# A hybrid decoder layer on one core: other banks and pools at the change from the attention loop to the merged projections, and the first fast pair as fourth unit

## The chip, the cores and the metric

The kernel runs on 1 core of one Trainium2 chip. The metric is the device time of one execution in microseconds. Before the change the median of 3 runs is 1044.36 us (1043.06 to 1044.58). The execution that the profiler recorded took 1042.83 us; its trace spans 1041.1 us from the first to the last instruction.

## The reference

One layer on 256 tokens of width 2048, all in float32. The input is normalised and projected to everything that follows; two token mixers, a 16-head latent attention and a short gated convolution, are widened by SiLU gates, projected back, weighted by two sigmoid gates that come from the input, added, and sent through one output projection:

```
h = _rmsnorm(x, pre_norm_g);  proj = h @ w_in      # q_a, c_kv, k_rope, z_mla, c_in, b_gate, c_gate, z_conv, g_mla, g_conv
attn   = causal_mla_attention(q, k, v) * silu(z_mla)
conv   = sum(conv_w[k] * u_pad[:, k:k + s] for k in range(3)),   u = c_gate * c_in
y_mla  = attn @ w_o_mla
y_conv = (b_gate * conv * silu(z_conv)) @ w_o_conv
merged = sigmoid(g_mla) * y_mla + sigmoid(g_conv) * y_conv
x + _rmsnorm(merged @ w_out, post_norm_g)
```

The change lies where the loop over heads ends and the four products with `g_mla`, `g_conv`, `w_o_mla` and `w_o_conv` begin. These four form the merged stage.

## The kernel before, in words

**Split operands.** Every float32 operand is used as two parts, a high part `hi` in the fast matmul format and the rest `lo`. A product of two such operands takes three matmuls (`product`, L262): hi by hi, hi by lo, lo by hi. The high part of a weight is a copy on ACT (`whi`), the low part a subtraction on DVE (`wlo`); both stand in `split_act` (L279). So TensorE (PE) waits for ACT and DVE, never for a transfer directly.

**Units.** The weights come in units of 1 MB in the order of a list. `load_raw` puts a unit in one of three `raw` tiles by a transfer on SP's queue, `split_unit` splits it, and `take(i)` runs loads three and splits one unit ahead. The split halves live in rings of five tiles each, `whi` and `wlo`; a unit takes two of each, so the copy of a later unit's half waits until PE has read an older one. ACT and DVE work strictly in the order in which their instructions stand. That order is set by a scheduler that gets the program as written, with the pools' overlaps as dependencies; transfers and PE's matmuls keep the program's order.

**The end of the loop over heads.** The last convolution block goes through a turn: DVE transposes a tile into `cw` or `mv2x`, POOL's queue writes it to `far` in DRAM and reads it back into `cv_f` (`turned`, L352; `channels_join`). These late transfers are still under way when the merged stage begins. The last head's values are summed in the bank with the tag "o" (`o15`), which DVE empties at L432 (`whole`), and the last convolution block in the two banks "cv".

**The merged stage.** It has four products n = 0..3 (two gates, two outputs), each in two column blocks c of eight pairs k of 128-row slices. A plain pair is four results by two slices, 8 products or 24 matmuls. Blocks with n < 2 go through `fast_block` (L1005), in which the pairs in `FAST = (0, 3, 5)` are computed in Strassen-Winograd form with 7 products, 21 matmuls, from sums of the operands: `split_seven` (L216) makes sums of the weights on DVE (`ts`, L222) and splits them (`th` on ACT, `tl` on DVE); `mixed(k)` (L984) makes sums of the normalised input (`xr` and `xm` on DVE, L988 and L992), split into `mix`. `first_sums` empties the banks that only fast pairs use (p1, q5, q7, q6), `last_sums` the others (p2, q3, q4, d22). The order of the first block is `pair_order[0, 0]` (L142): two plain pairs, 1 and 2, and then pair 0 as third unit.

**Space.** `bp`, the pool of the head loop, is closed (L949) and `sp` is opened over the same addresses: gates `g`, `mix`, the rings `ts`, `th`, `tl` and `ev` (whose tiles also hold `xr` and `xm`). A tile of `sp` may be written only when what lay there before is done. In the kernel before, the gates of n = 1 cover the two `cw` tiles and the `tl` ring covers `mv1x` and `mv2x`, the tiles of the late transfers.

In tile names the number behind `raw`, `whi`, `wlo`, `ts`, `th`, `tl` is that of the unit: 113 and 114 are the first two of the merged stage (pairs 1 and 2), 115 the third and so on.

Of the kernel before, what the change touches and what calls it, by code (L numbers as in the profile page):

```python
# [18 lines left out]
P = 128  # L19
S = 256  # L20
NT = S // P
D = 2048
# [62 lines left out]
def tile_layer(ctx: ExitStack, tc: tile.TileContext, xw, w0, xb, x, pos, pvec, post_g, wc, wz, wcv, wkr, wqk, wqr, wv, cwr, wd, wo, out):  # L85
# [53 lines left out]
            u_head[i][j] = add(wcv[i, j])  # L139

    pair_order = {(n, c): list(range(PAIRS)) for n in range(4) for c in range(2)}
    pair_order[0, 0] = [1, 2, 0, 4, 3, 6, 5, 7]  # L142
    u_d, seven = {}, set()
    for n in range(4):
        for c in range(2):
            for k in pair_order[n, c]:
                u_d[n, c, k] = add(wd[n, c, k])
                if n < 2 and k in FAST:
                    seven.add(u_d[n, c, k])

    out_order = [(c, k) for c in range(3) for k in range(2)] + [(c, k) for c in range(3) for k in (2, 3)]
# [64 lines left out]
    def split_seven(i, t):  # L216
        hi, hi2 = (wpool.tile([P, HALF], F32R, name=f"whi{i}_{j}", tag="whi", bufs=5) for j in range(2))
        lo, lo2 = (wpool.tile([P, HALF], F32R, name=f"wlo{i}_{j}", tag="wlo", bufs=5) for j in range(2))
        ta, tb = (sp.tile([P, HALF], F32, name=f"ts{i}_{j}", tag="ts", bufs=2) for j in range(2))
        ha, hb = (sp.tile([P, HALF], F32R, name=f"th{i}_{j}", tag="th", bufs=2) for j in range(2))  # L220
        la, lb = (sp.tile([P, HALF], F32R, name=f"tl{i}_{j}", tag="tl", bufs=2) for j in range(2))
        plus = lambda o, a, b: nc.vector.tensor_tensor(o, a, b, op=ALU.add)  # L222
# [36 lines left out]
    def bank(name, tag="mm", bufs=4):  # L259
        return psum.tile([P, 512], F32, name=name, tag=tag, bufs=bufs)  # L260
# [65 lines left out]
    bstack = main.enter_context(ExitStack())  # L326
# [17 lines left out]
    def temp(name, shape=(P, S), dt=F32, bufs=2, tag=None):  # L344

        tag, n = tag or name.rstrip("0123456789_"), shape[-1]
        if n % LINE == 0:
            return bp.tile(list(shape), dt, name=name, tag=tag, bufs=bufs)
        return bp.tile([P, -(-n // LINE) * LINE], dt, name=name, tag=tag, bufs=bufs)[:, :n]


# [597 lines left out]
    bstack.close()  # L949
    spool = ctx.enter_context(ExitStack())  # L950
    sp = spool.enter_context(tc.tile_pool(name="sp", bufs=1))
    gate = [[sp.tile([P, D], F32, name=f"g{n}_{t}") for t in range(NT)] for n in range(2)]
    mix = {k: sp.tile([P, 2, 4 * P], F32R, name=f"mix{k}") for k in FAST}

    def at_place(k):
        return x_both, k
# [25 lines left out]
            split_turned(src[:, c, t, :], place, c, t)  # L982

    def mixed(k):  # L984
        tmp = sp.tile([P, R], F32, name=f"xr{k}", tag="ev", bufs=2)
        f = tmp[:, :].rearrange("p (j s) -> p j s", j=2)
        ks = slice(2 * k, 2 * k + 2)
        nc.vector.tensor_tensor(f, x_both[:, ks, :S].bitcast(F32), x_both[:, ks, S:].bitcast(F32), op=ALU.add)  # L988
        raw = sp.tile([P, R], F32, name=f"xm{k}", tag="ev", bufs=2)
        a11, a21, a12, a22 = (f[:, j, t * P : (t + 1) * P] for j in range(2) for t in range(2))  # L990
        m7, m5, m6, m3 = (raw[:, j * P : (j + 1) * P] for j in range(4))
        minus = lambda o, a, b: nc.vector.tensor_tensor(o, a, b, op=ALU.subtract)  # L992
# [10 lines left out]
        return slice((2 * c + j) * R, (2 * c + j + 1) * R)  # L1003

    def fast_block(n, c, part, outs, between):  # L1005
        q = {name: bank(f"{name}_{n}{c}") for name in ("p1", "q5", "q7", "q6")}
        q["p2"] = bank(f"p2_{n}{c}", tag="st", bufs=1)
        q["q3"] = bank(f"q3_{n}{c}", tag="o", bufs=1)
        q["q4"], q["d22"] = (bank(f"{name}_{n}{c}", tag="cv", bufs=2) for name in ("q4", "d22"))
        order = pair_order[n, c]  # L1010
        calls = []
        for k in order:
            if k in FAST:
                for name, a, b in (
                    ("p1", part(2 * k, 0), "b11"), ("q5", mix_part(k, 1), "t1"), ("q7", mix_part(k, 0), "t3"),
                    ("q6", mix_part(k, 2), "t2"), ("p2", part(2 * k + 1, 0), "b21"), ("q3", mix_part(k, 3), "b22"),
                    ("q4", part(2 * k + 1, 1), "t4"),
                ):
                    calls.append((k, name, a, b))
            else:  # L1020
                for name, t, j in (("p2", 0, 0), ("q3", 0, 1), ("q4", 1, 0), ("d22", 1, 1)):
                    for i in range(2):
                        calls.append((k, name, part(2 * k + i, t), {(0, 0): 0, (1, 1): 1, (1, 0): 2, (0, 1): 3}[i, j]))
        firsts, lasts = {}, {}
        for at, (k, name, a, b) in enumerate(calls):
            firsts.setdefault(name, at)
            lasts[name] = at
        t_a, t_b = (sp.tile([P, R], F32, name=f"ev{i}_{n}{c}", tag="ev", bufs=2)[:, :] for i in range(2))
        (o11, o12), (o21, o22) = outs
        tt = lambda o, a, b, op=ALU.add: nc.vector.tensor_tensor(o, a, b, op=op)  # L1030

        def first_sums():
            nc.scalar.activation(t_a, q["p1"][:, :], AF.Copy)
            tt(t_b, q["q6"][:, :], t_a, ALU.subtract)
            tt(o12, q["q5"][:, :], t_b)
            tt(o21, q["q7"][:, :], t_b)
            tt(o22, q["q5"][:, :], o21)

        def last_sums():
            tt(o11, q["p2"][:, :], t_a)  # L1040
            tt(o12, q["q3"][:, :], o12)
            tt(o21, q["q4"][:, :], o21, ALU.subtract)
            tt(o22, q["d22"][:, :], o22)

        at = 0
        for i, k in enumerate(order):
            w = take(u_d[n, c, k])
            if i == order.index(max(FAST)) + 1:
                first_sums()
            between(i)  # L1050
            while at < len(calls) and calls[at][0] == k:
                _, name, a, b = calls[at]
                product(q[name][:, :], a, w[b] if k in FAST else w(b, R), firsts[name] == at, lasts[name] == at)
                at += 1
        last_sums()

    def plain_block(n, c, part, between):
        tags = ("mm",) * 4 if c == 0 else ("st", "o", "cv", "cv")
        q = {
            (t, j): bank(f"sq{n}{c}_{t}{j}", tag=tag, bufs={"mm": 4, "cv": 2}.get(tag, 1))  # L1060
            for (t, j), tag in zip(((0, 0), (0, 1), (1, 0), (1, 1)), tags)
        }
        order = pair_order[n, c]
        for at, k in enumerate(order):
            w = take(u_d[n, c, k])
# [10 lines left out]

    make_identity(nc, ident[:, :])
    for n in range(2):
        for c in range(2):

            def between(i):
                if n == c == 0 and i < 2:
                    for k in FAST[i : i + 1] if i == 0 else FAST[1:]:
                        mixed(k)
                if n == c == 1 and i in (2, 4, 6):
                    split_group(at_place, at_t, i // 2 - 1)

# [39 lines left out]
        for t in range(NT):  # L1127
            out_product(pss[t], t, w, kk)

    pss = [[bank(f"out{c}_{t}") for t in range(NT)] for c in range(2)]  # L1130
    pss.append([bank(f"out2_{t}", tag="cv", bufs=2) for t in range(NT)])
    for i, (c, kk) in enumerate(out_order[:6]):
        w = take(u_out[c, kk])
        if i == 5:
# [189 lines left out]
```

## Time and profile before

| | |
|---|---|
| median of the runs | 1044.36 us (1043.06 to 1044.58, 3 runs) |
| profiled execution | 1042.83 us, span 1041.1 us |
| busy share of the span | PE 98%, DVE 72%, ACT 52%, POOL 17% |
| mean granted TensorE clock | 0.993 |
| the chain that ended last | PE 97%, DVE 1% |

PE is busy to nine tenths or more in each of the page's 40 slices but two: the last (8 tenths) and one in the middle, from about 599 to 625 us (6 tenths), whose granted clock is 7 tenths. The merged stage begins at 590.09 us. "Idle before" in a row is the time in which the engine stood still ahead of an instruction; a matmul's row has its modelled length, and the distance between the starts of two rows is what it costs.

### The profile page before, as it was taken

How to read it: one execution, taken by the hardware profiler on the slowest of the kernel's cores; microseconds unless marked ns; L12 is line 12 of the kernel's file. 1: busy time of each engine (PE TensorE's matmuls, PEld its weight loads, DVE VectorE, ACT ScalarE, POOL GpSimd, SP SyncE). 2: the span in 40 equal slices, each digit the busy share in tenths (PEclk: the TensorE clock that was granted, in tenths of full speed). 3: DMA queues.
4: the chain of work that ended last, by engine and by line, in shares of the span. 5: the costliest groups of instructions: out<-in, count | busy, mean ns of one | idle time of the engine just before them, and what ended most of it. 6: DMA issues, size and time to landing. Idle time of an engine off the chain costs nothing.

```text
span 1041.1 us, 12831 instructions
## 1 busy us (share of the span) xinstructions
PE 1022.9 (98%) x4648; PEld 851.5 (82%) x4648; DVE 752.3 (72%) x1067; ACT 546.5 (52%) x766; POOL 179.8 (17%) x344
## 2 busy tenths in 40 slices
PE   9999999999999999999999969999999999999998
PEld 8888888888888888888888748888888888888886
DVE  7588777787777877777777789898975554657572
ACT  7666545555555555564555446555654343343451
POOL 4640421204211133012233110000000000214000
PEclk9999999999999999999999979999999999999999
DMA  9775876567665586656777635565645555577852
GB/s 358 281 246 213 273 223 226 203 213 270 228 234 208 206 265 225 248 212 204 267 241 259 226 122 196 204 218 190 229 173 198 202 195 184 207 263 252 327 189 81
DMA packets 44527, 233.26 MB, mean 224 GB/s; under 512 B 7952, under 2 KB 10512, under 8 KB 21552
## 3 DMA queue, kind: packets, MB, share of 16 engines
q1 hardware_dynamic: 32400, 199.67, 53.9%
q0 software_dynamic: 11632, 29.48, 8.8%
q10 hardware_dynamic: 432, 3.29, 0.8%
q8 instruction: 36, 0.59, 0.2%
q14 instruction: 27, 0.22, 0.1%
HBM read 215.66 MB, written 12.58 MB: 219 GB/s over the span
## 4 chain that ended last, share of the span: by engine, by line
PE 97%; DVE 1%; ACT 0%; DMA 0%; issue 0%; DVEq 0%
PE cv L90 34%; PE sq L90 17%; PE q L90 9%; PE z L90 8%; PE out L90 8%; PE p L90 4%; PE d L90 3%; PE qa L90 2%; PE kn L90 2%; PE qn L90 2%; PE vv L90 2%; PE ckv L90 2%; PE sc L90 1%; PE qr L90 1%; PE o L90 1%; PE kr L90 0%
## 5 line engine op out<-in xcount | busy, mean ns | idle before, releaser
L281 DVE TENSOR_TENSOR wlo<-raw,whi 128x1024 fp32r<-128x1024 f32 (+1 forms) x370 | 431.2, 1178 | 205.3 <-ACT whi L280 198.1
L280 ACT ACTIVATE whi<-raw 128x1024 fp32r<-128x1024 f32 (+1 forms) x372 | 373.1, 1020 | 375.7 <-PE cv L90 115.3
L90 PE MATMUL cv<-whi,x_both 128*128 128x512 f32 x1024 | 319.8, 389 | 0.0
L90 PEld LDWEIGHTS cv<-whi,x_both 128*128 128x128 f32 x1024 | 192.3, 188 | 39.5
L90 PE MATMUL cv<-wlo,x_both 128*128 128x512 f32 x512 | 199.5, 390 | 0.0
L90 PE MATMUL sq<-whi,x_both 128*128 128x512 f32 x384 | 118.7, 389 | 0.0
L90 PEld LDWEIGHTS cv<-wlo,x_both 128*128 128x128 f32 x512 | 96.1, 188 | 19.3
L90 PEld LDWEIGHTS sq<-whi,x_both 128*128 128x128 f32 x384 | 72.1, 188 | 15.0
L90 PE MATMUL z<-whi,x_both 128*128 128x512 f32 x256 | 80.0, 389 | 0.0
L90 PE MATMUL out<-whi,x_both 128*128 128x512 f32 x256 | 79.0, 389 | 0.0
L364 POOL DMA_DIRECT2D far<-g x32 | 17.5, 553 | 332.0 <-DVE g L1115 300.3
L90 PE MATMUL sq<-wlo,x_both 128*128 128x512 f32 x192 | 74.7, 389 | 0.0
L364 POOL DMA_DIRECT2D far<-via x64 | 35.3, 558 | 179.6 <-DVE via L356 179.6
L90 PEld LDWEIGHTS out<-whi,x_both 128*128 128x128 f32 x256 | 48.0, 188 | 10.1
L90 PEld LDWEIGHTS z<-whi,x_both 128*128 128x128 f32 x256 | 48.1, 188 | 9.9
L90 PE MATMUL q<-whi,x_both 128*128 128x512 f32 x160 | 52.6, 390 | 2.6 <-DVE f L432 2.6
L90 PE MATMUL z<-wlo,x_both 128*128 128x512 f32 x128 | 49.8, 389 | 0.0
L90 PE MATMUL out<-wlo,x_both 128*128 128x512 f32 x128 | 49.8, 389 | 0.0
L90 PE MATMUL p<-whi,x_both 128*128 128x512 f32 x128 | 47.0, 393 | 0.0
L90 PEld LDWEIGHTS sq<-wlo,x_both 128*128 128x128 f32 x192 | 36.0, 188 | 7.5
L364 POOL DMA_DIRECT2D far<-cw x48 | 26.2, 553 | 78.6 <-DVE cw L356 78.6
L90 PE MATMUL sq<-whi,cv_first 128*128 128x512 f32 x128 | 39.7, 389 | 0.0
(253 smaller groups left out, 1443.6 us busy)
## 6 DMA issues: line engine op xcount, KB each, us to landing
raw<-wcv_dram SPq DMA_DIRECT2D x64, 1024.0 KB, 5.6
raw<-wd_dram SPq DMA_DIRECT2D x64, 1024.0 KB, 4.8
raw<-wz_dram SPq DMA_DIRECT2D x16, 1024.0 KB, 4.8
raw<-wo_dram SPq DMA_DIRECT2D x16, 1024.0 KB, 4.8
raw<-wqk_dram SPq DMA_DIRECT2D x8, 1024.0 KB, 6.0
cw<-cwr_dram POOLq DMA_DIRECT2D x24, 256.0 KB, 6.2
raw<-wc_dram SPq DMA_DIRECT2D x4, 1024.0 KB, 9.7
raw<-wv_dram SPq DMA_DIRECT2D x4, 1024.0 KB, 4.9
```

The costliest lines, as they stand in the source:

```text
L90: return tc.keep_in_program_order(nc.tensor.matmul(*a, **kw))
L280: a = nc.scalar.activation(hi, src, AF.Copy)
L281: b = nc.vector.tensor_tensor(lo, src, hi.bitcast(F32), op=ALU.subtract)
L364: tc.keep_in_program_order(queue.dma_start(out=f[i], in_=m))
```

## The change

It does five things.

1. **Banks.** In `fast_block` the results p2, q3, q4 and d22, which plain pairs use, go to the four "mm" banks, and p1, q5, q7, q6 to "st", "o" and the two "cv". The plain blocks and the output blocks swap their banks to match.
2. **Order of the first block.** `pair_order[0, 0]` becomes 1, 2, 4, 0, 6, 3, 5, 7: pair 0 is the fourth unit, pair 3 the sixth.
3. **One fast pair less.** In that block pair 5 is plain: 24 matmuls where there were 21, and no `ts`, `th`, `tl` for it.
4. **Places.** `cw`, `mv1x` and `mv2x` get a pool `lp` of their own at the end of the space. In `sp` the rings `ts`, `th` and `ev` come first, over `qa`, `ckv` and other tiles that are done long before, the `tl` ring over tiles of the head loop. `g1_1` is opened over `lp` only at n = 1.
5. **Sums of the input.** `mixed` is called for pairs 0, 3, 5 at units 1, 3, 5 of the first block, where it was at units 0 and 1.

```diff
-    pair_order[0, 0] = [1, 2, 0, 4, 3, 6, 5, 7]
+    pair_order[0, 0] = [1, 2, 4, 0, 6, 3, 5, 7]
+    fast = {(n, c): FAST if n < 2 else () for n in range(4) for c in range(2)}
+    fast[0, 0] = FAST[:2]
...
-        ta, tb = (sp.tile([P, HALF], F32, name=f"ts{i}_{j}", tag="ts", bufs=2) for j in range(2))
+        ta, tb = (sums(f"ts{i}_{j}") for j in range(2))
...
+    lp = lstack.enter_context(tc.tile_pool(name="lp", bufs=1, side="right"))
...
-            return bp.tile(list(shape), dt, name=name, tag=tag, bufs=bufs)
+            return (lp if tag in ("cw", "mv1x", "mv2x") else bp).tile(list(shape), dt, name=name, tag=tag, bufs=bufs)
...
-    gate = [[sp.tile([P, D], F32, name=f"g{n}_{t}") for t in range(NT)] for n in range(2)]
-    mix = {k: sp.tile([P, 2, 4 * P], F32R, name=f"mix{k}") for k in FAST}
+    for r in (sums, sums_hi, evens):
+        r("home")
+    gate = [[None] * NT for _ in range(2)]
+    gate_tile(1, 0)
+    mix = {k: sp.tile([P, 2, 4 * P], F32R, name=f"mix{k}") for k in FAST[::-1]}
+    sums_lo("home")
+    for t in range(NT):
+        gate_tile(0, t)
...
-        q = {name: bank(f"{name}_{n}{c}") for name in ("p1", "q5", "q7", "q6")}
-        q["p2"] = bank(f"p2_{n}{c}", tag="st", bufs=1)
-        q["q3"] = bank(f"q3_{n}{c}", tag="o", bufs=1)
-        q["q4"], q["d22"] = (bank(f"{name}_{n}{c}", tag="cv", bufs=2) for name in ("q4", "d22"))
+        q = {name: bank(f"{name}_{n}{c}") for name in ("p2", "q3", "q4", "d22")}
+        q["p1"] = bank(f"p1_{n}{c}", tag="st", bufs=1)
+        q["q5"] = bank(f"q5_{n}{c}", tag="o", bufs=1)
+        q["q7"], q["q6"] = (bank(f"{name}_{n}{c}", tag="cv", bufs=2) for name in ("q7", "q6"))
...
-        tags = ("mm",) * 4 if c == 0 else ("st", "o", "cv", "cv")
+        tags = ("mm",) * 4 if c else ("st", "o", "cv", "cv")
...
+        if n:
+            lstack.close()
+            last_gate = spool.enter_context(tc.tile_pool(name="last_gate", bufs=1))
+            gate[1][1] = last_gate.tile([P, D], F32, name="g1_1")
...
-                if n == c == 0 and i < 2:
-                    for k in FAST[i : i + 1] if i == 0 else FAST[1:]:
-                        mixed(k)
+                if n == c == 0 and i in (1, 3, 5):
+                    mixed(FAST[i // 2])
...
-    pss = [[bank(f"out{c}_{t}") for t in range(NT)] for c in range(2)]
-    pss.append([bank(f"out2_{t}", tag="cv", bufs=2) for t in range(NT)])
+    pss = [[bank(f"out0_{t}", tag=tag, bufs=1) for t, tag in enumerate(("st", "o"))]]
+    pss += [[bank(f"out1_{t}", tag="cv", bufs=2) for t in range(NT)], [bank(f"out2_{t}") for t in range(NT)]]
```

Two places show how the instructions move. The first is ACT from the last convolution copy to the first `mix`, which PE waits for. Before, unit 115 is pair 0 (fast), 116 pair 4, 117 pair 3:

```order
L431 ACTIVATE half_5535<-o15_5529 128x256
L280 ACTIVATE whi115_1_5628<-raw115_5582 128x512
L280 ACTIVATE whi116_0_5692<-raw116_5625 128x1024
L280 ACTIVATE whi116_1024_5696<-raw116_5625 128x1024
L280 ACTIVATE whi117_0_5723<-raw117_5690 128x1024
L280 ACTIVATE th115_0_5633<-ts115_0_5631 128x1024
L280 ACTIVATE th115_1_5634<-ts115_1_5632 128x1024
L280 ACTIVATE mix0_5565<-xm0_5594 128x512
```

With the change unit 115 is pair 4 (plain), 116 pair 0 (fast), 117 pair 6, 118 pair 3:

```order
L434 ACTIVATE half_5538<-o15_5532 128x256
L282 ACTIVATE whi115_1024_5628<-raw115_5588 128x1024
L282 ACTIVATE whi116_0_5667<-raw116_5622 128x1024
L282 ACTIVATE whi116_1_5668<-raw116_5622 128x512
L282 ACTIVATE whi117_0_5714<-raw117_5665 128x1024
L282 ACTIVATE th116_0_5673<-ts116_0_5671 128x1024
L282 ACTIVATE whi117_1024_5718<-raw117_5665 128x1024
L282 ACTIVATE whi118_0_5754<-raw118_5712 128x1024
L282 ACTIVATE th116_1_5674<-ts116_1_5672 128x1024
L282 ACTIVATE mix0_5570<-xm0_5634 128x512
```

The two sums' copies stood together behind the first half of the unit after next; now two copies of later units stand between them, and `mix0` is behind all four.

The second place is DVE at the same point. Before, from the last low parts ahead of the sums of pair 0 to the first sum of the next fast pair; `xr3` and the low part of `mix0` follow:

```order
L281 TENSOR_TENSOR wlo116_1024_5697<-raw116_5625,whi116_1024_5696 128x1024
L281 TENSOR_TENSOR wlo117_0_5725<-raw117_5690,whi117_0_5723 128x1024
L988 TENSOR_TENSOR xr0_5592<-x_both_104 128x512
L222 TENSOR_TENSOR ts115_0_5631<-raw115_5582 128x1024
L992 TENSOR_TENSOR xm0_5594<-xr0_5592 128x128 x2
L222 TENSOR_TENSOR ts115_1_5632<-ts115_0_5631,raw115_5582 128x512
L992 TENSOR_TENSOR xm0_5594<-xr0_5592,xm0_5594 128x128
L222 TENSOR_TENSOR ts115_1_5632<-ts115_1_5632,raw115_5582 128x512
L281 TENSOR_TENSOR tl115_0_5635<-ts115_0_5631,th115_0_5633 128x1024
L992 TENSOR_TENSOR xm0_5594<-xr0_5592,xm0_5594 128x128
L281 TENSOR_TENSOR tl115_1_5636<-ts115_1_5632,th115_1_5634 128x1024
L222 TENSOR_TENSOR ts117_0_5727<-raw117_5690 128x1024
```

With the change, from the pass behind the last sum of `cv_f` to the first `xm0`:

```order
L283 TENSOR_TENSOR wlo115_1024_5629<-raw115_5588,whi115_1024_5628 128x1024
L283 TENSOR_TENSOR wlo116_0_5669<-raw116_5622,whi116_0_5667 128x1024
L359 STREAM_TRANSPOSE mv2_5551<-cv_f_108 128x4x4x32
L1008 TENSOR_TENSOR xr0_5632<-x_both_104 128x512
L224 TENSOR_TENSOR ts116_0_5671<-raw116_5622 128x1024
L1012 TENSOR_TENSOR xm0_5634<-xr0_5632 128x128 x2
```

Behind these stand `wlo116_1`, the first `ts116_1`, `wlo117_0` and a third `xm0`, and then, to the low part of `mix0`:

```order
L283 TENSOR_TENSOR tl116_0_5675<-ts116_0_5671,th116_0_5673 128x1024
L224 TENSOR_TENSOR ts116_1_5672<-ts116_1_5672,raw116_5622 128x512
L1012 TENSOR_TENSOR xm0_5634<-xr0_5632,xm0_5634 128x128
L224 TENSOR_TENSOR ts118_0_5758<-raw118_5712 128x1024
L283 TENSOR_TENSOR wlo117_1024_5719<-raw117_5665,whi117_1024_5718 128x1024
L1008 TENSOR_TENSOR xr3_5722<-x_both_104 128x512
L283 TENSOR_TENSOR wlo118_0_5756<-raw118_5712,whi118_0_5754 128x1024
L283 TENSOR_TENSOR tl116_1_5676<-ts116_1_5672,th116_1_5674 128x1024
L283 TENSOR_TENSOR mix0_5570<-xm0_5634,mix0_5570 128x512
```

`xr0` and the first sum of pair 0 stand ahead of the low parts of the next unit where they stood behind them; the late turn into `mv2` stands behind two low parts where it stood ahead of them; and two low parts and a `tl` now stand between the next fast pair's first sum and `mix0`. On PE the three matmuls more of pair 5 and the order of the pairs are all that moves; POOL's and SP's queues keep their order.

More of the change, by code (lines that the diff above doesn't have):

```diff
@@ L147, in tile_layer @@
                 u_d[n, c, k] = add(wd[n, c, k])
-                if n < 2 and k in FAST:
+                if k in fast[n, c]:
                     seven.add(u_d[n, c, k])
@@ L218, in split_seven @@
         lo, lo2 = (wpool.tile([P, HALF], F32R, name=f"wlo{i}_{j}", tag="wlo", bufs=5) for j in range(2))
-        ta, tb = (sp.tile([P, HALF], F32, name=f"ts{i}_{j}", tag="ts", bufs=2) for j in range(2))
-        ha, hb = (sp.tile([P, HALF], F32R, name=f"th{i}_{j}", tag="th", bufs=2) for j in range(2))
-        la, lb = (sp.tile([P, HALF], F32R, name=f"tl{i}_{j}", tag="tl", bufs=2) for j in range(2))
+        ta, tb = (sums(f"ts{i}_{j}") for j in range(2))
+        ha, hb = (sums_hi(f"th{i}_{j}") for j in range(2))
+        la, lb = (sums_lo(f"tl{i}_{j}") for j in range(2))
         plus = lambda o, a, b: nc.vector.tensor_tensor(o, a, b, op=ALU.add)
@@ L325, in tile_layer @@
     at_f = at_pool.tile([P, H, S], F32, name="at_f")
-    bstack = main.enter_context(ExitStack())
+    lstack, bstack = (main.enter_context(ExitStack()) for _ in range(2))
+    lp = lstack.enter_context(tc.tile_pool(name="lp", bufs=1, side="right"))
     bp = bstack.enter_context(tc.tile_pool(name="bp", bufs=1, side="right"))
@@ L951, in tile_layer, with ring, gate_tile @@
     sp = spool.enter_context(tc.tile_pool(name="sp", bufs=1))
-    gate = [[sp.tile([P, D], F32, name=f"g{n}_{t}") for t in range(NT)] for n in range(2)]
-    mix = {k: sp.tile([P, 2, 4 * P], F32R, name=f"mix{k}") for k in FAST}
+    def ring(tag, dt, size=HALF, bufs=2):
+        return lambda name: sp.tile([P, size], dt, name=name, tag=tag, bufs=bufs)
+    sums, sums_hi, evens, sums_lo = (
+        ring(tag, dt, size) for tag, dt, size in (("ts", F32, HALF), ("th", F32R, HALF), ("ev", F32, R), ("tl", F32R, HALF))
+    )
+    for r in (sums, sums_hi, evens):
+        r("home")
+    gate = [[None] * NT for _ in range(2)]
+    def gate_tile(n, t):
+        gate[n][t] = sp.tile([P, D], F32, name=f"g{n}_{t}")
+    gate_tile(1, 0)
[3 more added lines that the diff above has]
+        gate_tile(0, t)
     def at_place(k):
@@ L984, in mixed @@
     def mixed(k):
-        tmp = sp.tile([P, R], F32, name=f"xr{k}", tag="ev", bufs=2)
+        tmp = evens(f"xr{k}")
         f = tmp[:, :].rearrange("p (j s) -> p j s", j=2)
@@ L988, in mixed @@
         nc.vector.tensor_tensor(f, x_both[:, ks, :S].bitcast(F32), x_both[:, ks, S:].bitcast(F32), op=ALU.add)
-        raw = sp.tile([P, R], F32, name=f"xm{k}", tag="ev", bufs=2)
+        raw = evens(f"xm{k}")
         a11, a21, a12, a22 = (f[:, j, t * P : (t + 1) * P] for j in range(2) for t in range(2))
@@ L1005, in fast_block @@
     def fast_block(n, c, part, outs, between):
-        q = {name: bank(f"{name}_{n}{c}") for name in ("p1", "q5", "q7", "q6")}
-        q["p2"] = bank(f"p2_{n}{c}", tag="st", bufs=1)
-        q["q3"] = bank(f"q3_{n}{c}", tag="o", bufs=1)
-        q["q4"], q["d22"] = (bank(f"{name}_{n}{c}", tag="cv", bufs=2) for name in ("q4", "d22"))
-        order = pair_order[n, c]
+        q = {name: bank(f"{name}_{n}{c}") for name in ("p2", "q3", "q4", "d22")}
+        q["p1"] = bank(f"p1_{n}{c}", tag="st", bufs=1)
+        q["q5"] = bank(f"q5_{n}{c}", tag="o", bufs=1)
+        q["q7"], q["q6"] = (bank(f"{name}_{n}{c}", tag="cv", bufs=2) for name in ("q7", "q6"))
+        order, quick = pair_order[n, c], fast[n, c]
         calls = []
         for k in order:
-            if k in FAST:
+            if k in quick:
                 for name, a, b in (
@@ L1027, in fast_block @@
             lasts[name] = at
-        t_a, t_b = (sp.tile([P, R], F32, name=f"ev{i}_{n}{c}", tag="ev", bufs=2)[:, :] for i in range(2))
+        t_a, t_b = (evens(f"ev{i}_{n}{c}")[:, :] for i in range(2))
         (o11, o12), (o21, o22) = outs
@@ L1047, in fast_block @@
             w = take(u_d[n, c, k])
-            if i == order.index(max(FAST)) + 1:
+            if i == max(order.index(f) for f in quick) + 1:
                 first_sums()
@@ L1052, in fast_block @@
                 _, name, a, b = calls[at]
-                product(q[name][:, :], a, w[b] if k in FAST else w(b, R), firsts[name] == at, lasts[name] == at)
+                product(q[name][:, :], a, w[b] if k in quick else w(b, R), firsts[name] == at, lasts[name] == at)
                 at += 1
```

## The prediction

> **What bounds the kernel now.** First the page: span 1041.1 us, and a chain of waits that is PE to 97%. So only time in which PE stands still or runs slowly can be won. Then the waits of PE in the stretch around the one weak slice, and PE's timeline there (start, length, in brackets the idle time and what ended it):
>
> ```profile
> PE 97%; DVE 1%; ACT 0%; DMA 0%; issue 0%; DVEq 0%
> ```
>
> ```profile
> 590.09 0.39 PE L90 MATMUL p<-whi,x_both 128*128 128x512 f32 x1
> ...
> 591.24 0.40 PE L90 MATMUL p<-whi,x_both 128*128 128x512 f32 x1
> 594.21 0.50 PE L90 MATMUL q<-whi,x_both 128*128 128x512 f32 x1 [2.57 <-DVE f L432]
> ...
> 598.42 0.39 PE L90 MATMUL p<-whi,x_both 128*128 128x512 f32 x1
> ...
> 603.87 0.39 PE L90 MATMUL p<-whi,x_both 128*128 128x512 f32 x1
> ...
> 604.32 0.39 PE L90 MATMUL p<-whi,x_both 128*128 128x512 f32 x1
> 612.49 0.77 PE L90 MATMUL q<-th,mix 128*128 128x512 f32 x1 [7.78 <-issue]
> 613.05 0.63 PE L90 MATMUL q<-tl,mix 128*128 128x512 f32 x1
> 615.25 1.22 PE L90 MATMUL q<-th,mix 128*128 128x512 f32 x2 [1.57 <-DVE mix L281]
> ...
> 621.49 0.39 PE L90 MATMUL p<-whi,x_both 128*128 128x512 f32 x1
> ```
>
> A plain pair runs from 598.42 to 603.87: 24 matmuls in 5.45 us, 0.227 each. Measured from start to start and less one matmul, PE loses 594.21 - 591.24 - 0.227 = **2.74** us for the bank of q3 (tag "o"), which DVE empties late; 612.49 - 604.32 - 0.227 = **7.94** us for the high part of mix0; and 615.25 - 613.05 - 0.227 = **1.97** us for its low part. There is a fourth loss, the clock (columns: PE busy, PEld, DVE, ACT, POOL, granted clock, DMA share, GB/s):
>
> ```profile
> 590.00:597.00 7.00, 4.43 (x21) 3.36 (x20) 6.92 (x12) 1.63 (x3) 0.40 (x1) 1.00 0.43 152
> 604.50:606.90 2.40, 0.21 (x1) 0.00 (x0) 2.40 (x3) 0.89 (x1) 0.00 (x0) 1.00 0.34 77
> 606.90:620.50 13.60, 6.44 (x14) 4.63 (x15) 13.09 (x23) 4.90 (x6) 0.00 (x0) 0.50 0.40 148
> 620.55:624.00 3.45, 3.45 (x16) 2.82 (x15) 3.45 (x8) 2.02 (x3) 0.00 (x0) 1.00 0.23 28
> 622.00:680.00 58.00, 58.00 (x258) 48.00 (x257) 52.43 (x59) 36.04 (x41) 0.00 (x0) 1.00 0.57 199
> 680.00:1000.00 320.00, 320.00 (x1413) 265.00 (x1412) 214.60 (x230) 153.49 (x175) 21.92 (x40) 1.00 0.61 220
> ```
>
> From 606.90 to 620.50, 2.4 us into the long wait, PE is granted half its clock. The 18 matmuls from 612.49 to 621.49 take 9.00 us; at 0.227 they are 4.09, and 1.97 is the wait above, so the slow clock costs **2.94** us. Sum of the losses: 2.74 + 7.94 + 1.97 + 2.94 = **15.6 us**. The last two rows show that PE is never idle from 622 to 1000: nothing else is there to be won.
>
> Why was mix0 late? The timelines of ACT and DVE, and POOL's late transfers:
>
> ```profile
> 598.00 1.69 ACT L280 ACTIVATE whi<-raw 128x512 fp32r<-128x512 f32 x2 [6.38 <-PE d L90]
> 603.38 2.01 ACT L280 ACTIVATE whi<-raw 128x1024 fp32r<-128x1024 f32 x2 [3.69 <-PE d L90]
> 608.74 1.06 ACT L280 ACTIVATE th<-ts 128x1024 fp32r<-128x1024 f32 x1 [3.34 <-issue]
> ...
> 611.76 0.63 ACT L280 ACTIVATE mix<-xm 128x512 fp32r<-128x512 f32 x1 [0.28 <-DVE xm L992]
> ```
>
> ```profile
> 593.74 0.42 DVE L432 TENSOR_TENSOR f<-o,half 128x256 f32<-128x256 f32 x1
> ...
> 596.23 0.65 DVE L792 TENSOR_TENSOR cv_f<-cv_f,cv_w 128x512 f32<-128x512 f32 x1
> 596.92 0.71 DVE L356 STREAM_TRANSPOSE mv<-cv_f 128x512 f32<-128x512 f32 x1
> ...
> 604.48 2.36 DVE L281 TENSOR_TENSOR wlo<-raw,whi 128x1024 fp32r<-128x1024 f32 x2 [3.53 <-ACT whi L280]
> 606.75 0.69 DVE L988 TENSOR_TENSOR xr<-x_both 128x512 f32<-128x512 f32 x1
> 607.36 1.22 DVE L222 TENSOR_TENSOR ts<-raw 128x1024 f32<-128x1024 f32 x1
> 608.49 0.48 DVE L992 TENSOR_TENSOR xm<-xr 128x128 f32<-128x128 f32 x2
> 608.90 0.69 DVE L222 TENSOR_TENSOR ts<-ts,raw 128x512 f32<-128x512 f32 x1
> ...
> 614.51 0.69 DVE L281 TENSOR_TENSOR mix<-xm,mix 128x512 fp32r<-128x512 f32 x1
> ```
>
> ```profile
> 598.80 2.18 POOL L364 DMA_DIRECT2D far<-mv  x4
> ...
> 602.64 0.57 POOL L368 DMA_DIRECT2D cv_f<-far  x1 [1.10 <-DMA far<-mv]
> ```
>
> ```profile
> cv_f<-far POOLq DMA_DIRECT2D x2, 256.0 KB, 2.9
> ```
>
> ACT's copies into the `whi` ring wait for PE: they start when PE is 0.4 to 0.5 us short of the end of a unit (598.00 against 598.42, 603.38 against 603.87). DVE's low parts wait for these copies, and xr and ts stood behind them; their space also came free only about when the last late transfer landed (602.64 + 2.9 = 605.5). So the first sum began at 606.75.
>
> **The change part by part, on the clock of this trace.** *Banks:* q3 has an empty bank; nothing DVE still does stands ahead of it. The 2.74 us go: p1, q5, q7, q6 take "st", "o" and "cv" only at the fourth unit, over 10 us after DVE's pass at 593.74. In the later blocks both sets change places as wholes, so each bank is emptied as long ahead of its next use as before; the full rows from 622 to 1000 are the cover, and without it one eviction like that of q3, 2.74 us, would show.
>
> *One fast pair less:* 3 matmuls more, 3 x 0.227 = **+0.68** us, on the path. On ACT and DVE it takes work away (no ts, th, tl for that unit), off the path. The first sums now stand behind the sixth unit and not the seventh, so their four banks are empty two units ahead of the next block and not one.
>
> *Places:* xr and the sums no longer wait for the late transfers. The turn into mv2 moves behind two low parts, from 596.92 to about 599.2, and POOL's four writes and the read behind it with it; cv_f is read again only in the third product, four blocks on, and nothing else stands on POOL's queue until then. g1_1 waits for these transfers from the third block on, two blocks later; a block is about 5 x 5.45 + 3 x 21 x 0.227 = 42 us. SP's queue keeps its order. All at nothing; these distances are the cover, and where one fell short the wait would be that of one transfer, 2.9 us.
>
> *Order:* three plain units, from 590.09 without a stop: 590.09 + 3 x 5.45 = 606.44. Pair 0 begins with three matmuls of p1, which need neither sums nor mix: PE reaches the first use of mix0 at **607.1**. When is mix0 there?
>
> On ACT (by the order shown): whi117_1024, the second half of pair 6, needs a slot that the third unit gives back, so it starts 0.45 us short of its end, at 606.0. Then whi118_0, th116_1 and mix0. Two copies back to back take 2.01, so 0.95 from start to start: mix0 starts at 606.0 + 3 x 0.95 = 608.85 and ends 0.63 later. PE goes on at **609.55**: a wait of 2.45 us.
>
> On DVE: the sum of cv_f ends where its next pass began, at 596.9. From there to the low part of mix0 stand nine passes of 1024 columns, seven of 512 (mix0's included) and four xm; the copies that they need are ready in time (the closest is whi117_1024, done at 607.1, when DVE comes to it at 607.6). From start to start 1024 columns take 1.13 (607.36 to 608.49), 512 take 0.61 (606.75 to 607.36) and an xm 0.2 (608.49 to 608.90, two). 596.9 + 9 x 1.13 + 7 x 0.61 + 4 x 0.2 = **612.1**. PE has done two matmuls by 610.0 and waits until 612.15 or so: 2.2 us. DVE is busy without a gap over this stretch, so its own work, not a transfer, sets this wait.
>
> Bounds: the first wait is no less than 2.4, since the ring's slot is tied to PE itself, and no more than 3.6, if one pass of DVE ahead of th116_1 comes late. The second is 1.5 to 3.5, two DVE passes either way.
>
> *Clock:* not shown for two waits with two matmuls between. From below 0: around the wait of 2.57 us at 594.21 the clock was 1.00. From above 2.94, as after the long wait. I take **2.0**: 4.65 us idle with 0.45 us of work between them are nearer to the long wait, where the clock fell after 2.4 us, but PE is back to full work sooner.
>
> Sum: 2.45 + 2.2 + 2.0 + 0.68 = 7.3 where 15.6 were lost, so 8.3 us less than the profiled execution's 1042.83 us (span 1041.1): 1034.5. That execution is the fastest of the four known, 1.5 us under the median of 1044.36; where the slow clock sets in may be part of that spread, so I add a little and say **1034.8 us**.
>
> **The rivals.** *No slow clock.* Neither wait is as long as the 2.57 us that kept the clock at 1.00; then 2.0 us less, 1032.8. Against it: the fall after 2.4 us of the long wait. The Trainium skill, "TensorE: Matmul & The Clock Gate", HAM oscillation, asks for no idle gap over about 3.4 us; by that rule this rival holds. Part 1 of the same page has the clock fall after one idle window of 3.41 us that runs free: the slow stretch of 13.6 us is four such windows, which agrees, but its start 2.4 us into the wait does not agree with a whole idle window.
>
> *No wait at all.* If mix0 came by 607.1, 1042.83 - 15.6 + 0.68 = 1027.9. For it: xr can begin at 599.8, 7 us sooner. Against: the orders of ACT and DVE, each of which alone is late.
>
> *The late transfers still hold.* If the space of th116_0 came free only with the last of them (605.5, and 2.3 for the later turn: 607.8), th116_0 and the four copies behind it would follow: mix0 starts at 607.8 + 4 x 0.95 = 611.6 and PE goes on at 612.3, 5.2 us late; the second wait and a full slow clock behind it: 5.2 + 2.2 + 2.94 + 0.68 = 11.0, so 1038.2. Against: th now lies over ckv, read for the last time in the head loop.
>
> *Slower: the wait moves to the second fast pair.* The th ring has two tiles; th118_1 needs the one that PE reads until the last product of pair 0. If the pair of sums behind it misses the one plain unit in between, the hold of before, 7.94 + 1.97 + 2.94 = 12.85, comes a second time: 1034.5 + 12.85 = 1047.4. It decides from the point where one th and one tl pass (1.06 + 1.22) don't fit into 5.45 us of plain unit. Against: they do by half, and in the same arrangement before PE was not idle once from 622 to 680.
>
> **How the numbers follow.** A measurement of this kernel can tell 0.2%, 2.1 us. Forecast 0.70, no slow clock 0.14, no wait 0.06, transfers hold 0.06, slower 0.04. The bounds of the terms give 1042.83 - 15.6 + 0.68 + (2.4 + 1.5 + 0) = 1031.8 to 1042.83 - 15.6 + 0.68 + (3.6 + 3.5 + 2.94) = 1038.0; with a tenth left out on either side the range is 1032.2 to 1037.4. Four of the five cases are faster by over 0.2%: 0.94, with 0.02 taken off for a part of the last two: no change 0.02, slower 0.04.
>
> **What would show it.** Right: q3 starts 0.23 us behind p2; no idle time until the first q<-th,mix, which waits 2 to 3 us for ACT's mix and then again for DVE's; the granted clock drops to 0.5 for 7 us or less; PE's matmuls are 3 more. Wrong: an idle PE in a later block (the banks), a th that waits for a landing (the places), a wait at q<-th behind 622 (the second pair), or a mix that is there before PE asks.

## The result, and the profile after

The changed kernel takes 1034.05 us (median of 4 runs, 1033.29 to 1035.8), against 1044.32 us of the kernel before in the same rounds: a ratio of 0.9906, 95% interval 0.9889 to 0.9924. Forecast were 1034.8 us, between 1032.2 and 1037.4. The profiled execution took 1034.48 us, its span is 1032.7 us.

PE's timeline at the start of the merged stage and around the first fast pair (start, length, in brackets the idle time and what ended it):

```profile
591.38 0.40 PE L90 MATMUL p<-whi,x_both 128*128 128x512 f32 x1
591.62 0.39 PE L90 MATMUL q<-whi,x_both 128*128 128x512 f32 x1
...
606.59 0.39 PE L90 MATMUL p<-whi,x_both 128*128 128x512 f32 x1
...
607.04 0.39 PE L90 MATMUL p<-whi,x_both 128*128 128x512 f32 x1
609.74 0.77 PE L90 MATMUL q<-th,mix 128*128 128x512 f32 x1 [2.31 <-issue]
610.30 0.63 PE L90 MATMUL q<-tl,mix 128*128 128x512 f32 x1
612.31 1.22 PE L90 MATMUL q<-th,mix 128*128 128x512 f32 x2 [1.38 <-DVE mix L283]
...
617.92 0.39 PE L90 MATMUL p<-whi,x_both 128*128 128x512 f32 x1
```

q3 follows p2 without a stop (591.38, 591.62), where there were 2.74 us. The long wait has become one of 609.74 - 607.04 - 0.227 = 2.47 us and the second one 612.31 - 610.30 - 0.227 = 1.78 us. The 18 matmuls from 609.74 to 617.92 take 8.18 us; 4.09 of them are work and 1.78 the wait, so the slow clock costs 2.31 us. With the three matmuls more, 0.68, the losses are 7.24 us where they were 15.6. The difference, 8.4 us, is that of the two spans (1041.1 - 1032.7). The medians lie 10.3 us apart: the traced execution of the kernel before was faster than its four runs here, so about 2 us of the measured gain stand in no trace.

The same stretches as before, of the changed kernel (PE busy, PEld, DVE, ACT, POOL, granted clock, DMA share, GB/s):

```profile
607.00:609.40 2.40, 0.43 (x2) 0.01 (x1) 2.40 (x4) 2.40 (x4) 0.00 (x0) 1.00 0.92 271
609.50:616.30 6.80, 5.18 (x11) 3.65 (x12) 6.29 (x11) 1.72 (x3) 0.00 (x0) 0.50 0.54 227
616.40:622.00 5.60, 5.60 (x27) 4.61 (x25) 5.36 (x10) 3.28 (x4) 0.00 (x0) 1.00 0.42 136
622.00:680.00 58.00, 58.00 (x257) 48.06 (x256) 51.26 (x57) 33.31 (x38) 0.00 (x0) 1.00 0.55 195
680.00:1000.00 320.00, 320.00 (x1413) 265.06 (x1412) 212.91 (x226) 155.58 (x179) 21.86 (x40) 1.00 0.63 222
```

Half the clock is granted for 6.8 us, where it was 13.6. From 622 to 1000 PE has no idle time, as before: the swapped banks and the new places cost nothing there.

What sets the two waits stands in the timelines of ACT and of DVE, and POOL's late transfers:

```profile
606.17 2.00 ACT L282 ACTIVATE whi<-raw 128x1024 fp32r<-128x1024 f32 x2 [2.81 <-PE d L90]
608.08 1.04 ACT L282 ACTIVATE th<-ts 128x1024 fp32r<-128x1024 f32 x1
609.03 0.61 ACT L282 ACTIVATE mix<-xm 128x512 fp32r<-128x512 f32 x1
```

```profile
596.93 2.36 DVE L283 TENSOR_TENSOR wlo<-raw,whi 128x1024 fp32r<-128x1024 f32 x2
599.20 0.71 DVE L359 STREAM_TRANSPOSE mv<-cv_f 128x512 f32<-128x512 f32 x1
599.83 0.66 DVE L1008 TENSOR_TENSOR xr<-x_both 128x512 f32<-128x512 f32 x1
...
606.42 1.23 DVE L224 TENSOR_TENSOR ts<-raw 128x1024 f32<-128x1024 f32 x1
607.55 1.23 DVE L283 TENSOR_TENSOR wlo<-raw,whi 128x1024 fp32r<-128x1024 f32 x1
608.69 0.69 DVE L1008 TENSOR_TENSOR xr<-x_both 128x512 f32<-128x512 f32 x1
609.29 1.23 DVE L283 TENSOR_TENSOR wlo<-raw,whi 128x1024 fp32r<-128x1024 f32 x1
610.42 1.23 DVE L283 TENSOR_TENSOR tl<-ts,th 128x1024 fp32r<-128x1024 f32 x1
611.56 0.69 DVE L283 TENSOR_TENSOR mix<-xm,mix 128x512 fp32r<-128x512 f32 x1
```

```profile
604.09 1.16 POOL L371 DMA_DIRECT2D cv_f<-far  x2 [1.72 <-DMA far<-mv]
```

ACT stands 2.81 us, until PE gives back the slot for the second half of pair 6, and then does two copies, a th and mix0 in a row: the high part is there at 609.03 + 0.61 = 609.64. The view names no releaser for PE's first wait ("issue"); that it is this copy is read from the times, 609.64 and 609.74. DVE runs without a stop from 596.93 on and finishes the low part at 612.25. xr begins at 599.83, before the last late transfers are even issued.

### The profile page after: what moved, and what is told of

It reads as the page before. It is cut to its first block, busy times and chain, and to the rows that moved or that the text cites. A ratio compares the mean times of both kernels' runs of the same rounds, so it can differ in the third digit from the quotient of the medians.

```text
span 1032.7 us, 12827 instructions
## 1 busy us (share of the span) xinstructions
PE 1022.6 (99%) x4651; PEld 851.5 (82%) x4651; DVE 747.4 (72%) x1062; ACT 543.9 (53%) x764; POOL 179.0 (17%) x344
## 4 chain that ended last, share of the span: by engine, by line
PE 97%; DVE 2%; DMA 0%; ACT 0%; issue 0%
PE cv L90 34%; PE sq L90 17%; PE q L90 8%; PE z L90 8%; PE out L90 8%; PE p L90 4%; PE d L90 2%; PE kn L90 2%; PE qa L90 2%; PE qn L90 2%; PE vv L90 2%; PE ckv L90 2%; PE sc L90 1%; PE qr L90 1%; PE o L90 1%; DVE wlo L283 1%
## 5 line engine op out<-in xcount | busy, mean ns | idle before, releaser
L90 PE MATMUL q<-whi,x_both 128*128 128x512 f32 x168 | 55.1, 389 | 0.0
```

The lines of the kernel that those rows point to most:

```text
L90: return tc.keep_in_program_order(nc.tensor.matmul(*a, **kw))
```

## The experiments

Ten kernels were run, each timed four or five times beside the kernel before, whose medians were 1043.98, 1044.31 and 1043.88 us in the three groups (e1 to e4, e5 to e8, e9 and e10). The theory under test is the forecast's: the order on ACT and on DVE ahead of mix0 sets the waits. Its rivals are that the terms of the sum are independent gains, that the late transfers set the hold, and that the slow clock has another cause.

### e1: the banks alone

The kernel before, with p2, q3, q4, d22 in "mm" and the later blocks' banks swapped; order and places as before.

```diff
-        q = {name: bank(f"{name}_{n}{c}") for name in ("p1", "q5", "q7", "q6")}
+        q = {name: bank(f"{name}_{n}{c}") for name in ("p2", "q3", "q4", "d22")}
```

> The kernel before with the bank swap alone. Theory of the forecast (the hold at mix0 hangs on the whi ring, that is on PE's own progress): the wait for q3's bank, 2.74 us, goes, and the hold of 7.9 and 2.0 us stays as long as it was, 2.7 us earlier: 1044.3 - 2.7 = 1041.6, between 1041 and 1042.5. Rival (the late transfers' landing at 605.5 sets the hold): PE comes earlier and waits longer by as much, no gain, 1044.3.

Measured: 1039.38 us (1038.71 to 1039.91), ratio 0.9959 [0.9946, 0.9971]. The waits of PE in this kernel from 580 to 1000 us (total in us, how many, the longest):

```profile
PE q L90 <- ACT mix L280: 7.8, 1, 7.8
PE q L90 <- DVE mix L281: 1.6, 1, 1.6
```

The bank's wait is gone and the hold, the two waits at mix0, is of the same length to a hundredth (from start to start 7.94 and 1.98 us), though it begins 3 us earlier: the hold moves with PE and not with the transfers. The last late transfer is issued at 603.24 here, 0.6 us later than before, and xr begins at 603.79, 3 us earlier than before. The time is lower than the 1041 to 1042.5 expected: the gain, 4.6 us, is 1.9 more than the wait. The slow clock lasts 10.2 us in this kernel's trace and 13.6 in that of before; reckoned as above over the 18 matmuls it costs 1.80 us and not 2.94, so between the two traces it makes 1.1 us beside the wait's 2.74, of 4.2 in all. The expectation had left the slow clock as it was.

### e2: the changed kernel with the banks of before

The reverse of e1's edit, on the changed kernel.

```diff
-        q = {name: bank(f"{name}_{n}{c}") for name in ("p2", "q3", "q4", "d22")}
+        q = {name: bank(f"{name}_{n}{c}") for name in ("p1", "q5", "q7", "q6")}
```

> The changed kernel with the banks of before. If the terms of the sum add up, the wait for q3's bank comes back on top: 1034.05 + 2.74 = 1036.8. Rival (DVE's and ACT's work ahead of mix0 is the bound, and the bank only shifts where PE waits): PE comes 2.74 us later, mix0 is there, both waits of 2.47 and 1.78 us and the slow clock of 2.31 us go: the run's 1034.48 - 7.24 + 2.74 + 0.68 = 1030.7, up to 1031.7 where the bank's wait itself brings a slow clock. In this order of instructions th116_1 and mix0 stand ahead of whi117_1024 on ACT, which speaks for the rival.

Measured: 1031.22 us (1030.44 to 1032.24), ratio 0.9882 [0.9868, 0.9895]. Putting the bank's wait back makes the changed kernel **2.8 us faster**. PE's only wait from 580 to 1000 us, ACT's timeline, and the stretch behind the bank's wait in the table by stretches:

```profile
PE q L90 <- DVE f L435: 2.6, 1, 2.6
```

```profile
604.46 1.75 ACT L282 ACTIVATE whi<-raw 128x512 fp32r<-128x512 f32 x2 [2.42 <-PE d L90]
606.11 1.04 ACT L282 ACTIVATE th<-ts 128x1024 fp32r<-128x1024 f32 x1
607.05 0.61 ACT L282 ACTIVATE mix<-xm 128x512 fp32r<-128x512 f32 x1
609.96 2.01 ACT L282 ACTIVATE whi<-raw 128x1024 fp32r<-128x1024 f32 x2 [2.29 <-PE d L90]
```

```profile
593.40:596.70 3.30, 2.74 (x7) 2.17 (x8) 3.27 (x8) 0.00 (x0) 0.35 (x1) 0.50 0.34 142
```

PE stands 2.6 us for the bank, has half the clock for 3.4 us from just before the end of that wait, and then never waits for mix0: the scheduler, given another start, put mix0 ahead of the two copies that wait for PE, and it is done at 607.7. So the banks' term is no gain of its own in the changed kernel. PE has to wait for DVE's and ACT's work once; the swapped banks moved that wait to a later place and a worse order. How much of the 2.8 us is the order and how much the later arrival of PE, this run does not tell apart. The two copies that wait for PE start at 609.96, after mix0 is done: ahead of it, as in the changed kernel, they would have held it up again. The low part is done at 610.94 in this trace, 0.6 us before PE uses it, and there PE's later arrival helps. e8 gets as low without a wait for the bank.

### e3: the changed kernel with the places of before

cw, mv1x and mv2x in `bp`, `sp` laid out as before; banks, order and pair 5 as in the changed kernel.

```diff
-            return (lp if tag in ("cw", "mv1x", "mv2x") else bp).tile(list(shape), dt, name=name, tag=tag, bufs=bufs)
+            return bp.tile(list(shape), dt, name=name, tag=tag, bufs=bufs)
```

> The changed kernel with the pools of before (cw, mv1x, mv2x in bp, the rings last in sp). Theory: the space under ts, th and ev comes free only with the late transfers; the first wait grows from 2.5 to about 7.3 us, the second shrinks to 1.3, the slow clock costs 2.5 to 3: 1027.2 + 0.7 + 8.6 + 2 = 1038.5, between 1037 and 1040. Rival (the order of the units alone moves the sums ahead): no difference, 1034.

Measured: 1039.01 us (1038.1 to 1039.67), ratio 0.9954 [0.9941, 0.9966]. In DVE's timeline the sums' first instruction now waits for a transfer out of mv:

```profile
603.91 0.69 DVE L997 TENSOR_TENSOR xr<-x_both 128x512 f32<-128x512 f32 x1 [0.71 <-DMA far<-mv]
```

xr begins at 603.91 and not at 599.83. Only 0.71 us of this is the wait itself; two low parts that stand behind xr in the changed kernel are now ahead of it, so the places act through the order too. PE's first wait is 7.34 us from start to start, the second 0.84. The places are worth about 5 us (1039.01 - 1034.05): as expected.

### e4: the changed kernel with pair 0 as third unit

```diff
-    pair_order[0, 0] = [1, 2, 4, 0, 6, 3, 5, 7]
+    pair_order[0, 0] = [1, 2, 0, 4, 3, 6, 5, 7]
```

> The changed kernel with pair 0 as third unit again. Theory: PE comes 5.45 us earlier to the same work of DVE, so nearly all of that is added to the wait: first wait about 7.7, second 1.3, slow clock 2 to 3: 1027.2 + 0.7 + 9.0 + 2 = 1039, between 1037.5 and 1040.5. Rival (the places alone brought the gain): 1034.

Measured: 1038.71 us (1038.24 to 1039.19), ratio 0.9954 [0.994, 0.9968]. PE's first wait is 7.71 us and its second 0.91. The fourth place is worth 4.7 us, as expected. With the places or the order alone taken back, the kernel is within 0.7 us of e1, which has neither (1039.38). e1 still has pair 5 fast, 0.68 us less of matmuls, so either alone may be worth up to 1.4 us; together they bring about 5. The sums must be allowed to start early *and* PE must come late.

### e5: pair 5 fast again

```diff
-    fast[0, 0] = FAST[:2]
```

> The changed kernel with pair 5 of the first block fast again. By the count of matmuls 0.68 us less, 1033.4. Rival (ACT and DVE cannot make a third pair of sums in the time of this block): a wait of about 2.7 us at q6 of pair 5, and a part of a slow clock more: 1034.05 - 0.68 + 2.7 + 1 = 1037, between 1036 and 1038.

Measured: 1038.25 us (1037.17 to 1038.67), ratio 0.9943 [0.9929, 0.9957]. PE's timeline in pair 5:

```profile
629.14 0.63 PE L90 MATMUL q<-th,mix 128*128 128x512 f32 x2
632.01 0.50 PE L90 MATMUL q<-tl,mix 128*128 128x512 f32 x1 [2.24 <-DVE tl L282]
```

The three matmuls saved (0.68 us) are lost in a third wait, 632.01 - 629.14 less two matmuls = 2.4 us, and the trace shows a second slow stretch behind it, 3.4 us from 632.58 on. The plain pair 5 is worth about 4 us: 4.2 by the changed kernel's median, 3.7 by that of e6, timed in the same rounds. The expectation's sum, 1037, was 1.2 us low; the second slow clock had been put at 1 us.

### e6: mixed() called where it was

```diff
-                if n == c == 0 and i in (1, 3, 5):
-                    mixed(FAST[i // 2])
+                if n == c == 0 and i < 2:
+                    for k in FAST[i : i + 1] if i == 0 else FAST[1:]:
+                        mixed(k)
```

> The changed kernel with mixed() called where it was before (units 0 and 1). Theory: the order of instructions on every engine is the same as in the changed kernel, so no difference: 1033.3 to 1035.8, and the same waits of 2.5 and 1.8 us. Rival: xr and xm come earlier and take the first wait away: 1031.5.

Measured: 1034.59 us (1033.6 to 1034.99), ratio 0.9906 [0.9892, 0.992], the ratio of the changed kernel to the last digit. ACT's, DVE's and PE's instructions stand in the same order in both. This part of the change does nothing; the run also repeats the changed kernel beside e7 and e8.

### e7: matmuls of no use in the two waits

```diff
+                    fill = lambda m: [matmul(q["q7"][:, :], part(2 * k, 0)[0], w["b11"][0], start=True, stop=True) for _ in range(m)]
+                    fill(10)
                     matmul(q[name][:, :], ops[0][0], ops[1][0], start=True, stop=False)
                     matmul(q[name][:, :], ops[0][0], ops[1][1], start=False, stop=False)
+                    fill(8)
```

> The changed kernel; in the two waits of the first fast pair PE is given matmuls of no use, 10 ahead of the first product with mix0 and 8 between its second and third matmul, into a bank that the next product clears. They fit into the waits (10 x 0.227 = 2.27 of 2.47, 8 x 0.227 = 1.82 of 1.78). Theory: the slow clock comes from the two waits together; it goes, and nothing else changes: 1034.05 - 2.3 = 1031.8, and all runs close together, since where the slow clock sets in no longer matters. Rival (the clock falls for another reason, or the extra matmuls cost what they take): no gain, or up to 1036.

Measured: 1032.57 us (1031.72 to 1032.76), ratio 0.9888 [0.9873, 0.9904]. PE's timeline and the table by stretches:

```profile
605.69 0.39 PE L90 MATMUL p<-whi,x_both 128*128 128x512 f32 x1
...
606.37 2.43 PE L90 MATMUL q<-whi,x_both 128*128 128x512 f32 x10
608.84 0.47 PE L90 MATMUL q<-th,mix 128*128 128x512 f32 x1
609.15 0.40 PE L90 MATMUL q<-tl,mix 128*128 128x512 f32 x1
609.38 2.01 PE L90 MATMUL q<-whi,x_both 128*128 128x512 f32 x8
611.40 0.73 PE L90 MATMUL q<-th,mix 128*128 128x512 f32 x2
```

```profile
605.00:613.00 8.00, 7.94 (x34) 5.96 (x33) 8.00 (x13) 3.80 (x5) 0.00 (x0) 1.00 0.82 313
```

The third product with mix0 starts 611.40 - 605.69 = 5.71 us behind the pair's first matmul; in the changed kernel it is 612.31 - 606.59 = 5.72. The filling costs nothing, the clock stays whole, and 18 matmuls more make the kernel 2.0 us faster than e6, which is the same kernel without them (1.5 us by the changed kernel's own median). The profiled execution reached the stage 0.9 us earlier than that of the changed kernel; from there to the end the two take 440.6 and 442.5 us, 1.9 apart. So the slow clock comes from the two waits and is worth that.

### e8: the order held

The changed kernel with p2 ahead of q5, the splits of pair 0's sums and of mix0 held in the program's order, and mixed(5) two units later.

```diff
+        first_one = i == u_d[0, 0, 0]
+        split_act(ha[:, :], la[:, :], ta[:, :], first_one)
         split_act(hi[:, :], lo[:, :], t[:, :HALF])
+        split_act(hb[:, :], lb[:, :], tb[:, :], first_one)
         split_act(hi2[:, :R], lo2[:, :R], t[:, HALF : 3 * R])
-        split_act(ha[:, :], la[:, :], ta[:, :])
-        split_act(hb[:, :], lb[:, :], tb[:, :])
...
-        split_act(mix[k][:, 0, :], mix[k][:, 1, :], raw[:, :])
+        split_act(mix[k][:, 0, :], mix[k][:, 1, :], raw[:, :], k == 0)
...
-                if n == c == 0 and i in (1, 3, 5):
-                    mixed(FAST[i // 2])
+                if n == c == 0:
+                    for k in {1: (0,), 3: (3,), 7: (5,)}.get(i, ()):
+                        mixed(k)
```

> The changed kernel with three edits that go against its two waits: p2 of a fast pair stands ahead of q5 (three more matmuls that need no mix, 0.68 us of cover); the splits of pair 0's sums and of mix0 are held in the program's order, so that th116_1 and mix0 stand ahead of the next unit's copies on ACT and DVE; and mixed(5) is called two units later. Theory (the order on ACT and DVE is the bound, not their total work): the waits shrink to about 0.8 and 1.2 us, no slow clock: 1027.2 + 0.68 + 2.0 = 1029.9, between 1029 and 1031.5. Rival (DVE has no slack, so what is put ahead is paid behind, in the next units or at the start of the second block): 1033 to 1035.

Measured: 1030.92 us (1029.38 to 1032.36), ratio 0.9872 [0.9858, 0.9886]. PE's timeline and two stretches:

```profile
608.40 0.39 PE L90 MATMUL p<-whi,x_both 128*128 128x512 f32 x1
609.41 0.47 PE L90 MATMUL q<-th,mix 128*128 128x512 f32 x1 [0.62 <-issue]
610.90 0.50 PE L90 MATMUL q<-tl,mix 128*128 128x512 f32 x1 [1.02 <-DVE tl L284]
```

```profile
607.00:611.30 4.30, 2.66 (x11) 1.68 (x11) 3.42 (x6) 4.30 (x6) 0.00 (x0) 1.00 0.92 360
611.40:614.70 3.30, 3.30 (x9) 2.52 (x9) 3.30 (x4) 1.38 (x2) 0.00 (x0) 0.50 0.58 243
```

The waits are 0.78 and 1.26 us from start to start, the lengths expected, and nothing is paid behind them. The same instructions in another order, nearly all of it on ACT and DVE, bring over 3 us more: the order was the bound, not the amount of work. But the profiled execution, the slowest of the four, still has 3.4 us at half the clock, which the expectation had put at none. The other three spread from 1029.38 to 1031.05, the fastest of them at a mean clock of 0.999 and the two others at 1.000, so the clock does not explain that part.

### e9: p2 ahead of q5 alone

```diff
-                    ("p1", part(2 * k, 0), "b11"), ("q5", mix_part(k, 1), "t1"), ("q7", mix_part(k, 0), "t3"),
+                    ("p1", part(2 * k, 0), "b11"), ("p2", part(2 * k + 1, 0), "b21"), ("q5", mix_part(k, 1), "t1"),
```

> The changed kernel with one of the edits of e8 alone: p2 ahead of q5 in a fast pair. Theory: mix0 is no earlier, so three more matmuls lie under the first wait and nothing else changes: the first wait falls from 2.47 to about 1.8, the second stays near 1.8, the slow clock stays: 0.7 us less than the changed kernel, 1033.4, between 1032.5 and 1034.5. If it reaches e8's 1030.9, the cover and not the order of ACT and DVE did it there.

Measured: 1033.54 us (1033.07 to 1034.63), ratio 0.9904 [0.9891, 0.9918]. The first wait is 1.79 us and the second 2.03. The 0.5 us under the changed kernel's median fit the 0.68 expected, but lie inside both kernels' spread. Most of e8's gain is that of its other edits, the order held on ACT and DVE and the later mixed(5), which were not taken apart.

### e10: e8 with its waits filled

```diff
+                    fill(3)
                     matmul(q[name][:, :], ops[0][0], ops[1][0], start=True, stop=False)
+                    fill(5)
```

> The kernel of e8 with 3 and 5 matmuls of no use in its two waits of 0.78 and 1.26 us, into a bank that the next product clears. Theory (the slow clock falls when PE's busy share of one 3.41 us stretch is too small, however short each wait): all runs at full clock, lost are only 0.78 + 1.26 + 0.68: 1027.2 + 2.7 = 1029.9, all runs within 1 us. Rival (the slow clock in half of e8's runs has another cause): as e8, 1029.4 to 1032.4.

Measured: 1030.29 us (1029.67 to 1030.53), ratio 0.9872 [0.9858, 0.9885]. One row of its table by stretches:

```profile
600.00:622.00 22.00, 22.00 (x96) 17.31 (x95) 20.15 (x30) 12.99 (x16) 3.13 (x6) 1.00 0.60 218
```

The clock is whole and all runs lie within 0.9 us, as expected of the first theory; those of e8 lie within 3.0. As e8's spread is the clock's only in part, that the filling narrowed it is not shown. Against e8 the median is 0.6 us lower, which the intervals do not tell from none. e8, e10 and e2 beat both kernels; by the intervals they cannot be ranked among themselves.

## Why the prediction was right

*The bound.* That only PE's idle and slow time could be won holds: 15.6 us of losses became 7.24, and the spans differ by just that.

*Banks.* The 2.74 us went, and e1 shows the wait removed with order of pairs and places as before. What the step did not see is that in the changed kernel this is no gain: e2, with the wait put back, is 2.8 us faster. The sum of the whole was right because the two waits at mix0 were worked out with PE arriving that early; read as a worth of each part it would be wrong.

*One fast pair less.* +0.68 us on the path, as reckoned (4651 matmuls for 4648); what lies off the path, put at nothing, was worth more: e5, with pair 5 fast, is slower by 3.7 to 4.2 us. The forecast never priced the third wait that the plain pair 5 avoids.

*Places.* At nothing for the later blocks, right: no idle time from 622 to 1000. That xr would no longer wait for the late transfers is right (599.83), and e3 shows the wait that comes back. It is one for the write out of mv. The forecast had the space free only when the last read landed, about 605.5; in e1, with the old places, xr begins 0.55 us after that read is issued, where such a read took 2.9 us to land. So the landing was no bound; the low parts that stand ahead of xr on DVE were.

*Order.* Expected: whi117_1024 at 606.0, mix0 at 608.85, PE on again at 609.55, a wait of 2.45. Measured: 606.17, 609.03, 609.74, 2.47; this trace's stage starts 0.14 us later (590.23 against 590.09). DVE's passes were summed to 612.1 and ended at 612.25; the second wait was put at 2.2 and is 1.78, since the first matmul ran at half the clock (0.56 us for 0.227) and PE came 0.19 us later.

*Clock.* 2.0 taken, 2.31 measured in the trace; e7 gives 1.5 to 2.0 by medians. The 2.0 was a choice between 0 and 2.94, so it is luck in part that it came near, and also that its miss, 0.3 too low, and that of the second wait, 0.4 too high, nearly cancel. The rival *no slow clock* (1032.8) fell although neither wait is as long as the one that had left the clock whole. The rule of the Trainium skill ("TensorE: Matmul & The Clock Gate", HAM oscillation) of no idle gap over 3.4 us was kept and did not protect: here, with gaps of 2.47 and 1.78, and most plainly in e8.

*The other rivals.* PE did wait; no th waited for a landing in the changed kernel; the second fast pair brought no wait. So the step that failed is one of reading, not of the total: the 2.74 us of the banks as a gain of their own.

## What to carry to other kernels

When an engine in strict order feeds PE, look at what stands ahead of the late instruction, and whether that one waits for PE itself: here a copy that waits for a ring slot held up the one thing that PE wanted, and holding a few splits in place brought most of 3 us. A wait removed upstream is no gain while a queue downstream is the bound; undo each part by itself in the finished kernel, since one may now cost time. Where a wait cannot be removed, matmuls of no use that fit into it keep the clock.

## What the hardware showed

Half the clock came in stretches of one length or its multiples: 13.6 us before, 10.2 in e1, 6.8 in the changed kernel, 3.4 in e2 and e8. In each trace all changes of the clock lie on one grid of 3.413 us: before, the clock's record begins at 6.16 us, the clock falls 176 of these lengths later, at 606.90, and rises 4 lengths on, at 620.55. Where the grid lies differs from one execution to the next: the records begin at 3.8 to 6.6 us. So the fall came 2.4 us into the long wait before and 5.5 us into that of e4.

A long wait is not needed. The kernel before kept its clock through 2.74 us of idle time, and e2 lost it for 3.4 us after one of 2.73 at the same place; e8 lost it after 0.78 and 1.26 us with one matmul between. That fits a look at the end of each interval at how busy PE was in it, so that the same wait costs clock or not by where it falls: in the interval that took in the start of the bank's wait, PE was at work for 1.6 us before and for 1.3 in e2. Where the line lies is not shown: e4, too, had about 1.3 us of work in the interval in which its long wait began, and kept its clock to the next; e8 lost it after one with about 1.4.

The runs of the kernel before spread from 1042.4 to 1046.1 us in the first group, the fastest at a mean clock of 0.995 and the slowest at 0.990, which agrees. But not all spread is the clock's: the traces of e5 to e10, whose edits lie in the merged stage, reach that stage at 589.3 to 590.9 us.

The Trainium skill, "TensorE: Matmul & The Clock Gate", Part 1, has such a free-running window of 3.41 us, which agrees; that the clock falls only after an idle window, taken as one without work, does not agree with e8, where PE was at work for about 1.4 of the 3.4 us before the fall at 611.35: until 608.63, one matmul from 609.41, and again from 610.90.
